# Layer 0's output product by seven quarter products, with later weights rounded in half units

## The chip, the cores and the metric

One core of a Trainium2 chip runs the whole kernel. The metric is device time in microseconds: the median of three runs, 1159.79 us before the change (1158.65 to 1168.03). Engines are named as in the profile: PE multiplies matrices, DVE and ACT do the elementwise work, POOL does a little of it and issues DMAs, SP issues DMAs.

## What is computed

A decoder trunk of two layers over 512 tokens of 1024 features, in float32. Layer 0 mixes tokens with a state-space group and a stick-breaking attention group, layer 1 with a conformer convolution. Each mixer, and each feed-forward network (FFN) behind it, is added to a scaled residual and normalized:

```python
def sqrelu_mlp(x, w1, b1, w2, b2):
    return jnp.square(jax.nn.relu(x @ w1 + b1)) @ w2 + b2

        x = layer_norm(DEEPNORM_ALPHA * x + mix, ln1_g[layer], ln1_b[layer])
        ffn = sqrelu_mlp(x, ffn_w1[layer], ffn_b1[layer], ffn_w2[layer], ffn_b2[layer])
        x = layer_norm(DEEPNORM_ALPHA * x + ffn, ln2_g[layer], ln2_b[layer])
```

The FFN goes from 1024 to 4096 features and back. The change is in the FFN of layer 0 and in how weights of layer 1 are prepared meanwhile.

## The kernel before, in words

**Numbers.** Every operand of a matmul is held as a rounded high part and a low part (`hi`, `lo`; `split` casts on ACT and subtracts on DVE), and each product is three matmuls: high by high, high by low, low by high (`gemm`, L258). Features lie on partitions and tokens along the free axis; the residual `X[j]` is eight tiles of 128 × 512.

**FFN of layer 0, before.** It runs in four blocks of 8 hidden tiles (`FFN_BLOCKS[0]`). A hidden tile (`ffn1`; PSUM tile `f`, in the first block `fl`) is 24 matmuls of 512 columns; then Relu on ACT, a square on DVE and a split into `hh` and `hl`. After each of the first three blocks, `accum` makes 8 output tiles (`acf`) of 24 matmuls of 512 columns and adds them to `X`. The last block's output is made by `Tail` (`tlb`): 16 products of 24 matmuls of 256 columns, 8 output tiles for the first half of the tokens, 8 for the second, the weight of each output tile used in both halves.

**LN b.** `tail_norm_lead` weaves that tail with the layer norm behind it and with the first products of what follows (leads; here `pl`, four of the convolution's first pointwise product, `pw1`). Per token half: sums over the tiles (`sb`), their mean by a matmul with ones (`mpb`), subtraction, squares, sums of squares (`sqb`), their mean (`vpb`), scaling, and the split normalized tiles (`xbh`, `xbl`). The leads of a half follow. LN a, behind the mixer, has the same form with six leads (`fl`) that are the first hidden tiles of layer 0's FFN.

**Weights.** Class `Weights` prepares units (a raw load by SP, cast on ACT, L112, subtraction on DVE, L113) into slots in a fixed order, a few ahead of their use. 30 units of layer 1 (16 of `pw1`, 8 of `pw2`, 6 of the FFN's first matrix, 128 × 1024 each) are prepared in the same slots during layer 0's FFN and stored to DRAM by SP (`keep`: `kepth`, `keptl`); the convolution reloads them, split, through POOL's queue (L97).

**FFN of layer 1, before and after.** It has blocks of 6, 6, 6, 6 and 8 hidden tiles. For the blocks of six, `pair` turns two hidden tiles into seven operands `ah`, `al` (by token half and hidden tile of the pair), `load_quads` loads the output weights as four quarters (`quad`), `operand` forms their differences in place, and `seven` (L1400) makes seven quarter products in place of eight, in the order 1, 2, 5, 6, 3, 7, 4; some share a PSUM bank with the one that they are added to. `turn` closes the pools of the convolution and opens this layer's: slots `s1` to `s4`, `w` for the quarters, `a0` to `a2` for the operands, `q`. A tile of a new pool waits for the tiles that had its place.

**What sets the order.** The program is written in one order and a scheduler places each engine's instructions by priority; each engine then runs its own list strictly in order, and so does each DMA queue. Pages (`page`, 24 of 128 × 512) are taken in turn, and a page is given out again when its last reader is done.

Of the kernel before, what the change touches and what calls it, by code (L numbers as in the profile page):

```python
# [9 lines left out]
F32 = mybir.dt.float32  # L10
# [29 lines left out]
FFN_BLOCKS = ((8, 8, 8, 8), (6, 6, 6, 6, 8))  # L40
# [7 lines left out]
KEEP_FROM = 8  # L48
# [11 lines left out]
class Weights:  # L60


    def __init__(self, tc, ahead):
        self.tc, self.nc, self.ahead = tc, tc.nc, ahead
        self.slots, self.units, self.raw, self.urgent, self.fence, self.hold = [], [], None, True, None, False
        self.done, self.got, self.chunk, self.ready, self.kept = 0, 0, {}, {}, {}
        self.turn, self.quads, self.base = None, {}, 0
# [19 lines left out]
    def _prep(self, n):  # L87
        nc = self.nc
        while self.done < min(n, len(self.units)):
            key, src, nk, ncol, off, width = self.units[self.done]  # L90
            if self.turn and self.done == self.turn[0]:
                self.turn[1]()
            pool, s = self.slots[(self.done - self.base) % len(self.slots)]
# [12 lines left out]
            hi = pool.tile([P, nk, ncol], F32R, tag=f"whi{s}", name=f"whi{self.done}", bufs=1)  # L106
            lo = pool.tile([P, nk, ncol], F32R, tag=f"wlo{s}", name=f"wlo{self.done}", bufs=1)
# [33 lines left out]

    def keep(self, i):

        w = self.next()
        self.kept[i] = tuple(self.tc.dram_tile([P, *w[0].shape[1:]], F32, name=f"kept{x}{i}") for x in "hl")
        for x, d in zip(w, self.kept[i]):
            self.nc.sync.dma_start(d, x.bitcast(F32))
# [51 lines left out]
def kernel(ctx: ExitStack, tc: tile.TileContext, a: dict, out: bass.AP):  # L199
# [13 lines left out]
    X = [const([P, T], f"X{j}") for j in range(KT)]  # L213
# [49 lines left out]
    wst = ExitStack()  # L263
    wpool = wst.enter_context(tc.tile_pool(name="mw", bufs=1))
# [600 lines left out]
    wp2 = wst.enter_context(tc.tile_pool(name="w2", bufs=1))  # L865
    hst = ExitStack()
    hid = hst.enter_context(tc.tile_pool(name="hid", bufs=1, side="right"))
# [11 lines left out]
    def hpage(name, dt=F32R, w=T):  # L879
        return hid.tile([P, PAD + T + 2], dt, tag="hid", name=name, bufs=16)[:, :w]  # L880

    def tmp(name, dt=F32):
        return hid.tile([P, T], dt, tag="tmp", name=name, bufs=8)
# [6 lines left out]
    for j in range(0, D, 128):  # L890
        later += units_of("pw1", a["conv_w_pw1"][0], 0, 8, [j], 256)
        later += units_of("pw1", a["conv_w_pw1"][0], 0, 8, [D + j], 256)
    later += units_of("pw2", a["conv_w_pw2"][0], 0, 8, range(0, D, 128), 256)
    later += units_of("f1l", a["ffn_w1"][1], 0, 8, range(0, LEAD * P, 128), 256)

    kept = [k for j in range(0, 16, 4) for k in (j, j + 2, j + 1, j + 3)] + list(range(16, 24 + LEAD))
    keep_at, n = {}, 0
    for layer in range(2):
        if layer:
            units += [(("split", i), None, 8, 128, 0, 0) for i in range(24 + LEAD)]  # L900
            at_turn = len(W.units) + len(units)
        k0 = 0
        for nb in FFN_BLOCKS[layer]:
            if layer:
                units += units_of("f11", a["ffn_w1"][1], 0, 8, range(max(k0, LEAD) * P, (k0 + nb) * P, 128), 128)
                if nb == NB:
                    units += [(("quad", k0, i), None, nb // 2, T, 0, 0) for i in ORDER7]
                else:
                    for c in (0, T):
                        for k, n_ in ((0, 3), (3, 3), (6, 2)):  # L910
                            src = a["ffn_w2"][1][(k0 + k) * P : (k0 + k + n_) * P, c : c + T].rearrange("(k p) n -> p k n", p=P)
                            units.append((("f21", k0 + k, c), src, n_, T, 0, T))
                k0 += nb
                continue
            for m in range(k0, k0 + nb, 4):
                units += units_of("f10", a["ffn_w1"][0], 0, 8, range(m * P, min(m + 4, k0 + nb) * P, 128), 256)
                if m >= KEEP_FROM:
                    keep_at["f", m + 3] = kept[n : n + 2]
                    units += [later[i] for i in kept[n : n + 2]]
                    n += 2  # L920
            for j in range(0, KT, 4):
                units += units_of("f20", a["ffn_w2"][0], k0, nb, range(j * P, (j + 4) * P, 128), 256)
                if k0 + nb < 32:
                    m = 4 if j else 2
                    keep_at["a", k0, j + 3] = kept[n : n + m]
                    units += [later[i] for i in kept[n : n + m]]
                    n += m
            k0 += nb
    W.add_slots(wp2, 5)
# [78 lines left out]
    class Tail:  # L1008


        def __init__(self, xk, ln, bias):
            self.xk, self.ln, self.bias, self.done = xk, ln, bias, 0
            self.ws = [W.next() for _ in range(len(xk))]
            W.fence = None
# [51 lines left out]
    def tail_norm_lead(xk, name, bias, g, b, lead_n, lead_name, then=None, early=0):  # L1066

        ln = LN(name)
        t = Tail(xk, ln, bias)
# [10 lines left out]
    def ffn1(layer, bi, k0, nb, xs, fps, first=()):  # L1080
        hs = []
        for i in range(nb):
            m = k0 + i
            if i < len(first):
                ps = first[i]
            else:
                ps = fps(f"f{layer}{m}")
                gemm(ps, W.next(), slice(0, P), xs, 0, T)
# [3 lines left out]
            pg_ = page if (i < 4) == (bi % 2 == 0) else hpage  # L1092
            hh, hl = pg_(f"hh{layer}{m}"), pg_(f"hl{layer}{m}")
            split(hh, hl, r)
            hs.append((hh, hl))
            for k in keep_at.get(("f", m), ()) if layer == 0 else ():
                W.keep(k)
        return hs


# [6 lines left out]
    xs, first = tail_norm_lead(cat[4:8], "a", rb[0], ("ln1_g", 0), ("ln1_b", 0), LEAD, "fl0")  # L1107
    wdw = hid.tile([P, KT, CONV], F32, tag="wdw", name="wdw")
    mask = hid.tile([P, 32], F32, tag="mask", name="mask")

    def taps():
        for f in range(2):
            wn = tmp(f"wn{f}")[:CONV]
            nc.sync.dma_start(wn, a["conv_w_dw"][0][:, f * T : (f + 1) * T])
            ps = stp(f"wd{f}")
# [17 lines left out]

    acc = [None] * KT
# [380 lines left out]
```

## Time and profile before

| | us |
|---|---|
| median of three runs | 1159.79 |
| profiled execution, its time | 1164.9 |
| span of the profiled execution | 1163.2 |
| PE busy | 1133.7 |
| DVE busy | 820.6 |
| ACT busy | 550.0 |

The mean granted clock of PE was 0.994. The time of the profiled execution is 1.7 us over its span, which runs from the first to the last recorded instruction. Busy times overlap between engines; what PE's busy time leaves of the span, 29.5 us, is all the time in which no matmul ran. In the views of the profile, `L258` is a line of the kernel before, an arrow in `out<-in` stands between what an instruction writes and reads, and `x192` counts instructions.

### The profile page before, as it was taken

Reading aid. Unit: us, or ns where it says so; the run is one execution under the profiler, and the core shown is the slowest. Engines: PE = TensorE matmul, PEld = TensorE weight load, DVE = VectorE, ACT = ScalarE, POOL = GpSimd, SP = SyncE. Lnnn points to the kernel's source line nnn. Section 1 sums busy time; section 2 is a strip of 40 time slices with the busy share of each in tenths; the row PEclk is TensorE's granted clock in tenths of the full one; section 3 lists DMA queues with packets and bytes.
Section 4 is the critical chain, followed back from the end, with each engine's and each line's share of the span. In section 5 each row is a group of like instructions: output and inputs, shape, how many; then the busy total and the mean of one; then the engine's idle time right before and its main releaser. Section 6 shows DMA issues by size and latency. Waiting matters only on the chain.

```text
span 1163.2 us, 17835 instructions
## 1 busy us (share of the span) xinstructions
PE 1133.7 (97%) x7156; PEld 948.5 (82%) x7156; DVE 820.6 (71%) x1401; ACT 550.0 (47%) x838; POOL 70.2 (6%) x125
## 2 busy tenths in 40 slices
PE   9989989999999999999999999999999999999997
PEld 7777767799888888888899867689988888888885
DVE  7999865578645645645647699988695958588337
ACT  7857759435524524523513231364673536263530
POOL 1022221000000000000002211002000000000000
PEclk9999989999999999999999999999999999999999
DMA  9621212150878778788617634156024151515211
GB/s 204 173 63 50 74 56 74 55 181 14 267 244 289 250 273 282 267 268 274 217 46 245 226 137 146 39 170 227 4 82 135 50 151 44 172 35 156 65 54 73
DMA packets 145907, 169.59 MB, mean 146 GB/s; under 512 B 13922, under 2 KB 119138, under 8 KB 145824
## 3 DMA queue, kind: packets, MB, share of 16 engines
q1 hardware_dynamic: 137024, 136.96, 37.1%
q0 software_dynamic: 8640, 31.46, 8.0%
q8 instruction: 56, 0.92, 0.3%
q14 instruction: 27, 0.22, 0.1%
q10 hardware_dynamic: 160, 0.03, 0.0%
HBM read 132.12 MB, written 35.65 MB: 144 GB/s over the span
## 4 chain that ended last, share of the span: by engine, by line
PE 78%; DMA 6%; DVE 6%; ACT 5%; issue 2%; SPq 2%; POOL 1%; DVEq 0%; ACTq 0%
PE f L258 20%; PE acf L258 10%; PE s L1400 10%; DMA raw<-in_ffn_w_dram 4%; PE tld L258 4%; PE h L1445 4%; PE tlb L258 4%; PE fl L258 3%; PE pv L258 3%; PE cw L1174 3%; PE pg L258 3%; PE tla L258 2%; PE acmo L258 2%; DVE wlo L113 2%; PE pl L258 2%
## 5 line engine op out<-in xcount | busy, mean ns | idle before, releaser
L112 ACT CAST whi<-raw 128x1024 fp32r<-128x1024 f32 (+1 forms) x150 | 156.6, 1061 | 259.1 <-PE acf L258 66.3
L113 DVE TENSOR_TENSOR wlo<-raw,whi 128x1024 fp32r<-128x1024 f32 (+1 forms) x150 | 183.6, 1236 | 122.1 <-ACT whi L112 122.1
L258 PE MATMUL f<-xah,whi 128*128 128x512 f32 x208 | 81.0, 390 | 0.0
L258 PE MATMUL f<-xal,whi 128*128 128x512 f32 x208 | 81.0, 389 | 0.0
L258 PE MATMUL f<-xah,wlo 128*128 128x512 f32 x208 | 80.9, 389 | 0.0
L258 PE MATMUL f<-xdh,whi 128*128 128x512 f32 x208 | 80.9, 389 | 0.0
L258 PE MATMUL f<-xdl,whi 128*128 128x512 f32 x208 | 80.9, 389 | 0.0
L258 PE MATMUL f<-xdh,wlo 128*128 128x512 f32 x208 | 80.9, 389 | 0.0
L258 PE MATMUL acf<-hl,whi 128*128 128x512 f32 x192 | 75.8, 395 | 0.1
L258 PE MATMUL acf<-hh,wlo 128*128 128x512 f32 x192 | 75.7, 394 | 0.0
L258 PE MATMUL acf<-hh,whi 128*128 128x512 f32 x192 | 75.3, 392 | 0.0
L1400 PE MATMUL s<-whi,al 128*128 128x512 f32 x168 | 65.0, 390 | 0.0
L1400 PE MATMUL s<-wlo,ah 128*128 128x512 f32 x168 | 64.9, 390 | 0.0
L1400 PE MATMUL s<-whi,ah 128*128 128x512 f32 x168 | 64.5, 392 | 0.0
L113 DVE TENSOR_TENSOR wlo<-quad,whi 128x1536 fp32r<-128x1536 f32 x28 | 49.1, 1754 | 7.6 <-ACT whi L112 7.5
L391 DVE SCALAR_TENSOR_TENSOR cy<-hp,wdw,cy 128x512 f32<-128x512 f32 (+1 forms) x75 | 49.5, 660 | 0.5 <-ACT cy L187 0.5
L112 ACT CAST whi<-quad 128x1536 fp32r<-128x1536 f32 x28 | 41.0, 1483 | 17.2 <-PE f L258 8.0
L97 POOL DMA_DIRECT2D whi<-kepth x30 | 16.0, 535 | 547.6 <-PE tlb L258 386.7
L258 PEld LDWEIGHTS f<-xdh,whi 128*128 128x128 f32 x208 | 39.0, 188 | 8.1
L258 PEld LDWEIGHTS f<-xah,wlo 128*128 128x128 f32 x208 | 39.0, 188 | 8.1
L258 PEld LDWEIGHTS f<-xah,whi 128*128 128x128 f32 x208 | 39.0, 188 | 8.1
L258 PEld LDWEIGHTS f<-xdl,whi 128*128 128x128 f32 x208 | 39.0, 188 | 8.1
(647 smaller groups left out, 3064.4 us busy)
## 6 DMA issues: line engine op xcount, KB each, us to landing
raw<-in_ffn_w_dram SPq DMA_DIRECT2D x35, 1024.0 KB, 6.0
kepth<-whi SPq DMA_DIRECT2D x30, 512.0 KB, 4.4
keptl<-wlo SPq DMA_DIRECT2D x30, 512.0 KB, 9.5
whi<-kepth POOLq DMA_DIRECT2D x30, 512.0 KB, 3.6
wlo<-keptl POOLq DMA_DIRECT2D x30, 512.0 KB, 4.4
raw<-in_ffn_w_dram SPq DMA_DIRECT2D x28, 512.0 KB, 4.0
raw<-in_conv_w_pw_dram SPq DMA_DIRECT2D x12, 1024.0 KB, 6.7
quad<-in_ffn_w_dram SPq DMA_DIRECT2D x16, 768.0 KB, 4.6
```

Source lines behind the costliest of these rows:

```text
L97: nc.gpsimd.dma_start(x, d)
L112: i0 = nc.scalar.copy(hi, raw).ins
L113: i1 = nc.vector.tensor_sub(lo, raw, hi.bitcast(F32)).ins
L258: ins = PE.matmul(ps[:, c0:c1], u[:, k, ksl], v[:, c0:c1], start=start and k == 0 and i == 0, stop=stop and k == n - 1 and i == 2).ins
L391: V.scalar_tensor_tensor(o, x, s, y, op0=op0, op1=op1)
L1174: PE.matmul(cps[j, c0][g][C, :], Ds[j][t // 16][R, t % 16, :], hps[j][R, t + c0 : t + c1], start=t < 4, stop=t >= n - 4, tile_position=(R. ...
L1400: PE.matmul(ps, u, v[:, p, :], start=chain == i and p == 0 and n_ == 0, stop=p == len(As) - 1 and n_ == 2, skip_group_check=True)
L1445: PE.matmul(ps, u, v, start=k == 0 and i == 0, stop=k == nb_last - 1 and i == 2)
```

## The change

Layer 0's FFN takes the blocks of layer 1, 6, 6, 6, 6 and 8, and its first four blocks the seven products.

- **Products.** `seven_by_feature` makes them with the weights as the stationary operand, so that the result comes out with features on partitions, in PSUM tiles `z` of 128 × 512 that hold two feature tiles of one token half: per block 7 × 36 = 252 matmuls of 256 columns. The first block's product 1 starts a sum `R1` (two pages) that is added to half of `X` during the last block; the other results are added to `X` directly (`region`).
- **Hidden tiles.** `pair` serves both layers; Relu and Square write `q` in place on ACT. The last block's hidden tiles go to the places of `a0` to `a2`.
- **Pools.** `quarters(0)` opens layer 0's pools behind LN a; `plain`, called when the first unit of the convolution's weights is prepared, lays `tmp one hid four two three` over them, with 12 tiles in `tmp`. `tmp` (sums and squares of LN b among them) begins where `s1` and `s2` lie. The first four output weights of the last block are put into places of `w` and `q` (`in_quads`, `in_q`), the other four into the slots.
- **Later weights.** `half_units` loads the 30 later units in 60 halves of 256 KB into pages (`kr`), splits them (`kh`, `kl`) and stores both parts, all three DMAs issued by POOL. `keep` does one half: 7 in the first block, 13 in each of the next three, 14 in the last.
- **Residual.** `X` is scaled and gets its bias in eight ACT instructions ahead of the FFN, instead of the bias in each addition; the transposes of the convolution's taps (`taps`) are taken in two steps of block 0.

The core of the diff:

```diff
+    def half_units():
+        raws = {}
+        def load(n):
+            if n < 2 * (24 + LEAD):
+                (w, c), h = later[n // 2], n % 2
+                raws[n] = page(f"kr{n}", F32)
+                G.dma_start(raws[n].rearrange("p (k n) -> p k n", k=4), w[4 * h * P : 4 * (h + 1) * P, c : c + P].rearrange("(k p) n -> p k n", p=P))
+        load(0)
+        for n in range(2 * (24 + LEAD)):
+            load(n + 1)
+            hi, lo = page(f"kh{n}"), page(f"kl{n}")
+            split(hi, lo, raws.pop(n))
+            for d, x in zip(W.kept[n // 2], (hi, lo)):
+                G.dma_start(d[:, 4 * (n % 2) : 4 * (n % 2) + 4, :], x.bitcast(F32).rearrange("p (k n) -> p k n", k=4))
+            yield
...
-            r = tmp(f"fr{layer}{m}")
-            act(r, ps, AF.Relu, bias=pv("ffn_b1", 32 * layer + m))
-            tt(r, r, r, ALU.mult)
...
+            ps = pss[e] if pss else hidden(layer, m + e, xs)
+            x = q[:, 1:3] if e else q[:, 0:8:7]
+            act(x, ps.rearrange("p (h c) -> p h c", h=2), AF.Relu, bias=pv("ffn_b1", 32 * layer + m + e))
+            act(x, x, AF.Square)
+            if then:
+                then()
...
+    ORDERS = ("s1 s2 raw s3 a1 s4 a2 a0 q w", "s1 s2 raw w a1 s4 a2 b q s3 a0")
...
+    def plain():
+        wst[0].close()
+        wst[0] = ExitStack()
+        p = opened("tmp one hid four two three".split())
+        room.update(tmp=p["tmp"], hid=p["hid"], bufs=12)
+        W.slots, W.count, W.raw, W.ahead = [], 0, None, 5
+        for x, n in (("three", 3), ("two", 2), ("one", 1), ("four", 4)):
+            W.add_slots(p[x], n)
...
+    for j in range(KT):
+        act(X[j], X[j], AF.Identity, bias=rb[1][:, j : j + 1], scale=ALPHA)
+    R1 = [page(f"R1{b}", F32) for b in range(2)]
...
+    def seven_by_feature(k0, As, first, bi):
+        bank, opened = {}, None
+        for n, i in enumerate(ORDER7):
+            wh, wl = W.next()
+            chain = CHAIN.get(i, i)
+            for b in range(2):
+                if chain == i:
+                    bank[i, b] = nps(f"z{k0}{i}{b}")
+                ps = bank[chain, b]
+                for d in range(2):
+                    c = slice((2 * b + d) * P, (2 * b + d + 1) * P)
+                    for p, (ah, al) in enumerate(As):
+                        uh, ul = ah[:, PLACE[i]], al[:, PLACE[i]]
+                        for n_, (u, v) in enumerate(((wh, uh), (wh, ul), (wl, uh))):
+                            opens = chain == i and p == 0 and n_ == 0
+                            ins = PE.matmul(ps[:, d * H : (d + 1) * H], u[:, p, c], v, start=opens and d == 0,
+                                            stop=p == len(As) - 1 and n_ == 2, skip_group_check=True).ins
...
+            for b in range(2):
+                ps = bank[chain, b]
+                if i == 1:
+                    if first:
+                        S.copy(R1[b], ps)
+                    else:
+                        tt(R1[b], R1[b], ps, ALU.add)
+                else:
+                    x = region({2: 0, 5: 3, 6: 1, 3: 1, 7: 3, 4: 2}[i], b)
+                    tt(x, x, halves(ps), ALU.add)
+            keep()
...
-    for bi, nb in enumerate(FFN_BLOCKS[0]):
-        if bi == 1:
-            taps()
-        hs = ffn1(0, bi, k0, nb, xs, nps, first if bi == 0 else ())
-        if bi < len(FFN_BLOCKS[0]) - 1:
-            accum(nps, hs, f"f0{bi}", 1024 // nb, bi == 0, keep=lambda j: keep_at.get(("a", k0, j), ()))
+    for bi, nb in enumerate(FFN_BLOCKS[:-1]):
+        if bi:
+            W.load_quads(k0, a["ffn_w2"][0], k0, nb)
+        As = []
+        for m in range(k0, k0 + nb, 2):
+            As.append(pair(0, m, xs, first[m : m + 2] if bi == 0 else None, keep if bi else None))
+        seven_by_feature(k0, As, bi == 0, bi)
         k0 += nb
-    xs, first = tail_norm_lead(hs, "b", rb[1], ("ln2_g", 0), ("ln2_b", 0), 4, "pl")
+    hs, ws = [], []
+    for i in range(FFN_BLOCKS[-1]):
+        if i % 3 == 0:
+            hl_ = [f1[f"a{i // 3}"].tile([P, 3, T], F32R, tag=f"a{x}", name=f"h0{x}{i}", bufs=1) for x in "hl"]
+        r = rect(0, k0 + i, hidden(0, k0 + i, xs))
+        act(r, r, AF.Square)
+        hs.append(tuple(x[:, i % 3, :] for x in hl_))
+        split_part(*hs[-1], r)
+        if i < 4:
+            ws.append(W.next())
+        x = region(i // 2, i % 2)
+        tt(x, x, halves(R1[i % 2]), ALU.add)
+        keep(2 - (i > 5))
+    xs, first = tail_norm_lead(hs, "b", None, ("ln2_g", 0), ("ln2_b", 0), 4, "pl", ws=ws)
```

How the instructions stand on the engines, at three places. A number behind a name (`tlb_5603`) tells one tile from another, and lines are those of the kernel that the rows are of. First PE around LN b, before the change: the last product ahead of the first half's mean and the first behind it, and the same for the variance.

```order
L258 MATMUL tlb_5603<-hh_5315,wlo_5211 128x256
L956 MATMUL mpb_5629<-sb_5423,ones 128x256
L258 MATMUL tlb_5662<-hh_5037,whi_5246 128x256
...
L258 MATMUL tlb_5717<-hh_5315,wlo_5320 128x256
L956 MATMUL vpb_5744<-sqb_5632,ones 128x256
L258 MATMUL tlb_5776<-hh_5037,whi_5329 128x256
```

PE there in the change, from the end of the tail's last product on:

```order
L257 MATMUL tlb_6748<-h0h_6118,whi_6210 128x256
L257 MATMUL tlb_6748<-h0l_6119,whi_6210 128x256
L257 MATMUL tlb_6748<-h0h_6118,wlo_6211 128x256
L982 MATMUL mpb_6520<-sb_6314,ones 128x256
L982 MATMUL vpb_6635<-sqb_6523,ones 128x256
L257 MATMUL pl_6775<-xbh_6478,whi_6242 128x256
L257 MATMUL pl_6833<-xbh_6478,whi_6246 128x256
```

Before, 216 tlb products stand ahead of `mpb`, 72 between it and `vpb`, and 96 behind that; in the change all 384 stand ahead of both.

Second, DVE in the first half of LN b, before the change: the tail's evacuations (`X<-tlb`) and the sums `sb`.

```order
L391 SCALAR_TENSOR_TENSOR X_61<-tlb_5371,rb_2541,X_61 128x256
L391 SCALAR_TENSOR_TENSOR X_62<-tlb_5397,rb_2541,X_62 128x256
L387 TENSOR_TENSOR sb_5423<-X_61,X_62 128x256
L391 SCALAR_TENSOR_TENSOR X_63<-tlb_5425,rb_2541,X_63 128x256
L387 TENSOR_TENSOR sb_5423<-sb_5423,X_63 128x256
```

And in the change; `tlb_6721` and `tlb_6748` are the tail's 15th and 16th products, `D` diagonals of the convolution.

```order
L387 TENSOR_TENSOR X<-tlb_6694,X 128x256
L387 TENSOR_TENSOR X<-tlb_6721,X 128x256
L1332 TENSOR_TENSOR D_7040<-mask,wdw 128x512
L1332 TENSOR_TENSOR D_7041<-mask,wdw 128x256
L387 TENSOR_TENSOR sb_6314<-X 128x256
L387 TENSOR_TENSOR X<-tlb_6748,X 128x256
L387 TENSOR_TENSOR sb_6314<-sb_6314,X 128x256
L1307 MEMSET hp_7044 128x30
L387 TENSOR_TENSOR sb_6314<-sb_6314,X 128x256 x5
L387 TENSOR_TENSOR X<-X,mpb_6520 128x256 x8
```

The first sum stood behind the second evacuation and stands now behind the 15th; the other six stand behind the 16th.

Third, DVE at the start of block 0 in the change; `q` and `al` belong to the operands of the last pair, `wlo` from a `quad` is one of the seven weight operands, `kl` a half unit.

```order
L387 TENSOR_TENSOR q_3426<-q_3426 128x256
L1207 COPY wdw<-wd_3496 128x124
L118 TENSOR_TENSOR wlo_3223<-quad_3214,whi_3222 128x1536
L118 TENSOR_TENSOR wlo_3227<-quad_3216,whi_3226 128x1536
L138 TENSOR_TENSOR quad_3214<-quad_3218,quad_3214 128x1536
L1120 TENSOR_TENSOR al_3428<-q_3426,ah_3427 128x768
L387 TENSOR_TENSOR q_3426<-q_3426 128x256
L142 TENSOR_TENSOR quad_3218<-quad_3220,quad_3218 128x1536
L118 TENSOR_TENSOR wlo_3232<-quad_3214,whi_3231 128x1536
```

All seven weight operands and the four differences stand behind the last pair's first difference, which needs the last lead's square.

More of the change, by code (lines that the diff above doesn't have):

```diff
@@ L211, in page @@
         return pgp.tile([P, T], dt, tag="pg", name=name, bufs=24)
[L213 removed]
+    Xall = const([P, KT, T], "X")
+    X = [Xall[:, j, :] for j in range(KT)]
     ident = const([P, P], "ident")
@@ L890 @@
     for j in range(0, D, 128):
[L891 to L897, printed above, removed]
-    for layer in range(2):
+        later += [(a["conv_w_pw1"][0], c) for c in (j, D + j)]
@@ L902 @@
[L902 to L927, printed above, removed]
-            k0 += nb
@@ L1078, in tail_norm_lead, with rect @@
         return xs, lead.finish()
[L1080 to L1088, printed above, removed]
-            r = tmp(f"fr{layer}{m}")
-            act(r, ps, AF.Relu, bias=pv("ffn_b1", 32 * layer + m))
-            tt(r, r, r, ALU.mult)
[L1092 to L1098, printed above, removed]
+    def rect(layer, m, ps):
+        r = page(f"r{layer}{m}", F32)
+        act(r, ps, AF.Relu, bias=pv("ffn_b1", 32 * layer + m))
+        return r
@@ new lines, with opened, quarters, turn @@
+    PLACE = {1: 0, 2: 1, 4: 2, 5: 3, 6: 4, 7: 5, 3: 6}
+    CHAIN = {3: 5, 7: 6, 4: 6}
+    f1 = {}
+    wm = ExitStack()
+    ORDERS = ("s1 s2 raw s3 a1 s4 a2 a0 q w", "s1 s2 raw w a1 s4 a2 b q s3 a0")
+    def opened(names, **kw):
+        return {x: wst[0].enter_context(tc.tile_pool(name=f"{x}{len(W.units)}{W.done}", bufs=1, reuse_waits="tile", **kw)) for x in names}
+    def quarters(layer):
+        def turn():
+            if layer:
+                wm.close()
+            wst[0].close()
+            wst[0] = ExitStack()
+            room.clear()
+            f1.clear()
+            f1.update(opened(ORDERS[layer].split()))
+            W.slots, W.count, W.raw, W.ahead = [], 0, f1["raw"], NSLOT - 1
+            for x in ("s1", "s2", "s3", "s4"):
+                W.add_slots(f1[x], 1)
+            W.quad = f1["w"]
+            W.load_quads(0, a["ffn_w2"][layer], 0, NB)
+        return turn
```

185 lines of the change are left out of this document (113 added, 72 removed).

## The prediction

> **What bounds the kernel now.** I read the page first, then the chain of waits, then windows over single stages, then the rows of LN b and of the costs.
>
> ```profile
> span 1163.2 us, 17835 instructions
> PE 1133.7 (97%) x7156; PEld 948.5 (82%) x7156; DVE 820.6 (71%) x1401; ACT 550.0 (47%) x838; POOL 70.2 (6%) x125
> ```
>
> PE is busy for 97% of the span: only 29.5 us are without a matmul. So whatever takes products away shortens the kernel only if no new idle time of PE appears, and whatever makes PE wait counts in full.
>
> ```profile
> 401.94 44.59 PE acf L258 x192
> 446.53 43.52 PE f L258 x192
> ...
> 582.37 22.52 PE tlb L258 x187
> 604.89 0.43 PE mpb L956 x2
> 605.32 8.56 PE tlb L258 x72
> 613.89 0.43 PE vpb L956 x2
> 614.32 11.42 PE tlb L258 x96
> 625.73 2.88 PE pl L258 x24
> ...
> 639.32 11.09 PE pl L258 x92
> 650.41 5.24 PE pv L258 x23
> ```
>
> Each row is start, duration, engine, tile, line, count. In layer 0's FFN the chain runs through PE row upon row: a hidden block (f), an output block (acf), a hidden block. In LN b, mean (mpb) and variance (vpb) of the first token half lie between tlb products of the second half, and the leads (pl) of the first half follow at once: the norm's first half is hidden under the tail.
>
> ```profile
> 358.00:402.00 44.00, 44.00 (x197) 36.41 (x196) 27.55 (x33) 22.65 (x29) 0.00 (x0) 1.00 0.84 285
> 578.00:626.00 48.00, 47.06 (x392) 46.69 (x391) 29.36 (x69) 9.68 (x21) 7.64 (x15) 1.00 0.42 143
> 883.00:945.00 62.00, 62.00 (x274) 50.95 (x273) 45.68 (x49) 29.10 (x32) 0.00 (x0) 1.00 0.35 103
> ```
>
> The columns after the stretch and its length are busy time of PE, weight loads, DVE, ACT and POOL, the granted clock, the DMA share and GB/s. PE is full in a hidden block of layer 0 (row 1), in the tail with 256-column products (row 2, where weight loads are nearly full as well), and in a seven-product block of layer 1 (row 3). The others have room; DVE has least of it, in row 3, the pattern that layer 0 now takes over.
>
> **The change, part by part.** First, the products. Removed are three acf blocks of 192 matmuls of 512 columns, by the chain's row 44.59 each: 133.8 us. Added are four blocks of 252 matmuls of 256 columns. Their nearest rows are the tlb rows: (22.52 + 8.56 + 11.42) / (187 + 72 + 96) = 0.1197 us each; 1008 × 0.1197 = 120.7. Hidden products, tail and leads keep their number. PE work falls by **13.1 us**, and this can't be more than 16.8, which half a 512-wide matmul (0.2322 / 2) would make of it; the weight loads, one to a matmul in row 2, speak against that.
>
> Second, LN b. By the order of the change the first sum of LN b's first half (sb) comes on DVE behind the 15th of 16 tlb evacuations, and PE issues all 384 tlb before mpb. The sum's tile lies where the weight of the tail's seventh tile lies, which is read once more by the 15th product. So the norm's first half can't lie under the second half of the tail. Its length stands in the second half of before, where nothing covered it:
>
> ```profile
> 626.29 0.42 DVE L387 TENSOR_TENSOR sb<-sb,X 128x256 f32<-128x256 f32 x1
> 629.08 2.73 DVE L387 TENSOR_TENSOR X<-X,mpb 128x256 f32<-128x256 f32 x8 [2.37 <-PE mpb L956]
> 631.74 2.55 DVE L387 TENSOR_TENSOR sqb<-sqb,sqb 128x256 f32<-128x256 f32 x7
> 635.89 0.42 DVE L391 SCALAR_TENSOR_TENSOR tb<-vpb,rb 128x256 f32<-128x256 f32 x1 [1.60 <-ACT rb L193]
> 637.27 1.28 DVE L391 SCALAR_TENSOR_TENSOR X<-X,PV,rb 128x256 f32<-128x256 f32 x3
> ...
> 628.45 0.59 PE L956 MATMUL mpb<-sb,ones 128*128 128x256 f32 x2
> 638.35 0.74 PE L258 MATMUL pl<-xbh,whi 128*128 128x256 f32 x4 [0.26 <-ACT xbh L187]
> ```
>
> The chain from mpb (628.45) to the first lead of that half (638.35) takes 9.9 us. Call the end of the last tlb T. After T follow, in the change, one evacuation at 0.42, six sums that depend on each other at 0.42 (some 3 us with their starts), then the 9.9, and 1.1 more for the second half's sums that DVE does in between, with 0.9 for the two hand-overs: the first lead starts at T + 14.9, and PE has nothing to do until then. 96 lead products at 0.12 are 11.5, so they end at T + 26.4. The clock adds to that:
>
> ```profile
> 159.45 1.12 PE L757 MATMUL av<-w2C,vt 128*64 128x256 f32 x2 [4.41 <-POOL w2C L706]
> 160.00:162.00 2.00, 1.17 (x4) 0.29 (x2) 0.00 (x0) 0.38 (x1) 0.29 (x1) 0.50 0.00 0
> 164.00:168.00 4.00, 4.00 (x25) 3.55 (x24) 1.12 (x4) 3.42 (x7) 0.39 (x2) 0.72 0.00 0
> ```
>
> After 4.41 us of idle PE the granted clock is 0.50, and its mean over 164 to 168 still 0.72: 1.1 us are lost in these four, and about as much before; I take 1.9, so T + 28.3. The second half's mpb, behind the first half's chain on DVE (its last rows end near T + 20.9), has the same 9.9 behind it: T + 30.8 for the first lead of that half, and with another 11.5 and its start T + 42.9 for the last. Before, this took from 625.73 to 650.41, 24.7. The loss is **18 us**; at the least 15 (the uncovered chain alone, the second half hidden whole), at the most 22.
>
> The Trainium skill (TensorE: Matmul & The Clock Gate, section Part 1: The HAM clock gate) has the clock fall after a window of about 3.4 us without work. By this rule the second gap of LN b, 2.5 us, keeps the full clock and my sum stands; by the row alone, which shows only a longer gap, it may fall again and cost another 1.9.
>
> Third, the start of block 0. The order puts 32 DVE instructions between the first weight split and product 7's first evacuation, behind the last lead's square. Their prices:
>
> ```profile
> L113 DVE TENSOR_TENSOR wlo<-raw,whi 128x1024 fp32r<-128x1024 f32 x146 | 176.6, 1222 | 107.2 <-ACT whi L112 107.1
> L113 DVE TENSOR_TENSOR wlo<-quad,whi 128x1536 fp32r<-128x1536 f32 x28 | 49.1, 1754 | 7.6 <-ACT whi L112 7.5
> L249 DVE TENSOR_TENSOR hl<-fr,hh 128x512 fp32r<-128x512 f32 x32 | 22.0, 689 | 12.4 <-ACT hh L248 12.4
> L387 DVE TENSOR_TENSOR X<-X,s 128x512 f32<-128x512 f32 x48 | 31.9, 682 | 11.9 <-PE s L1400 11.9
> L137 DVE TENSOR_TENSOR quad<-quad,quad 128x1536 f32<-128x1536 f32 x4 | 7.0, 1756 | 0.1
> L1367 DVE TENSOR_TENSOR al<-q,ah 128x1024 fp32r<-128x1024 f32 x12 | 14.7, 1222 | 6.7 <-ACT ah L1366 6.7
> L187 ACT ACTIVATE X<-X,rb 128x512 f32<-128x512 f32 x16 | 10.2, 719 | 0.0
> ```
>
> Seven operand splits 12.3, four operand differences 7.0, two raw splits 2.4, two parts of al 2.2, nine evacuations 6.1, five half units (kl, priced as hl) 3.4, three short differences 1.3: 34.8 us. Product 4 follows on PE with 4.3, so the block ends 39.1 after DVE's start; PE has 252 × 0.1197 = 30.2 of its own, and 9 products of the next block that it does meanwhile (2.1). That leaves 6.8 of waiting. I take **6**, since the queue can start a little ahead of PE; from 0 (PE itself late by its last pair, DVE ahead) to 10 (the operands' loads late too). The eight scalings of X on ACT (0.72 each, in the leads) are within it.
>
> Fourth, the later weights. What moves:
>
> ```profile
> kepth<-whi SPq DMA_DIRECT2D x30, 512.0 KB, 4.4
> whi<-kepth POOLq DMA_DIRECT2D x30, 512.0 KB, 3.6
> ...
> 880.00:890.00 10.00, 10.00 (x45) 8.29 (x45) 4.09 (x6) 2.59 (x4) 0.00 (x0) 1.00 0.46 132
> 1050.00:1060.00 10.00, 10.00 (x46) 8.29 (x45) 10.00 (x14) 2.84 (x3) 0.00 (x0) 1.00 0.77 244
> 520.00:530.00 10.00, 10.00 (x45) 8.12 (x44) 3.51 (x5) 2.10 (x2) 0.00 (x0) 1.00 0.99 372
> ```
>
> 60 stores of 512 KB leave SP; 60 half loads and 120 half stores of 256 KB come to POOL's queue, ahead of the 60 reloads there, which are needed only from LN b on. The same bytes are cast and subtracted, in pieces of 512 columns. In blocks 1 to 3, 13 pieces each add 13 × 0.689 = 9.0 to DVE's 45.7 of row 3: 54.7 of some 63 us, so PE's products hide them. A piece holds three of six free pages from its load to the end of its stores; at about 3.7 us each, 13 take 48, hidden as well. In the last block the cover is thin: eight hidden tiles are 43.5 us on PE, 16 weights of 0.524 MB and 14 loads of 0.262 are 12.06 MB, by row 880 (132 / 0.46 = 287 GB/s with rows of 512 bytes) 42 us, and 28 stores of 0.262 by row 520 (372 / 0.99 = 376) 20: 62. Of these some 16 may lie ahead or behind (the first weights are preloaded, the tail's last ones and stores come later), so 46 against 43.5. And the last hidden tile's split stands on DVE behind the last piece's: a late load or page there holds the tail. I take **5 us**, from 0 (all hidden) to 20 (the 62 in full, with the next block's start).
>
> The Trainium skill (DMA: Bandwidth & Descriptors, section Specifications) counts rows of 512 bytes as enough for full rate. By this the loads go as fast as the wider rows at 1050 (244 / 0.77 = 317 GB/s), the last block's transfers fit under its products, and the sum is about 3 lower; the trace has 287, and I keep to it.
>
> R1's additions in the last block (8 of 0.68) lie under hidden products, Relu and Square in place cost ACT what the separate ones did.
>
> **Sum**: −13.1 + 18 + 6 + 5 = **+15.9**. The profiled execution took 1164.9 (span 1163.2), so it would take 1180.8; it lies 5.1 over the median of the three runs, and on the median 1159.79 the forecast is **1175.7 us**, slower by 1.4%.
>
> **Rivals.** A: the only new wait is LN b's uncovered chain at its least, 15, and block 0 and the pieces hide: −13.1 + 15 = +1.9, **1161.7 us**, no change. For it: ACT and the DMA queues have much room, and layer 1 runs the same blocks with PE full (row 883). Against: in layer 1 there are no pieces, and other work covers the first operands. B: pieces and weights bind in the last block, by DMA or by pages: the fourth term at 20, +30.9, **1190.7 us**. For it: one queue issues 180 transfers, in order, each waiting for its page or its split. Against: the rate of 376 at row 520 shows reserves. C, the other side: the sums do not wait, and run tile by tile under the tail as before. What decides is whether the sum's tile must be free of the seventh weight. Since PE's own order has no tlb behind mpb, mpb then comes at T, the first lead at T + 10.5 (0.6 and 9.9), the second half's first at T + 23, and the last at T + 35.5: the loss shrinks from 18 to 10.8, and with block 0 and the pieces hidden the time is 1159.8 − 13.1 + 10.8 = **1157.5**, not slower; with z at its lower bound 1153.8. For it: order shows rows and not waits. Against: the sum's first row stands behind the 15th evacuation there, where before it stood behind the second.
>
> **Chances.** Forecast 0.45, A 0.28, B 0.19, C 0.08. A difference of 1% (11.6 us) is about what a measurement of this kernel can tell. Of the forecast's 0.45, with its own bounds, 0.39 lies over 1171.4 and 0.06 below; A gives 0.26 to no change and 0.02 to slower, B all to slower, C 0.05 to no change and 0.03 to faster, this if the second half's chain hides too. Faster 0.03, same 0.37, slower 0.60. The range is 1160 to 1197: it takes in most of A and all of B but its end, and leaves out C (0.08), A's lower part (0.08) and the worst of B (0.04).
>
> **What would show it.** Right, if in the profile after z takes about 0.12 us a matmul; if tlb runs in one piece of 384 and PE is then idle for about 15 us, with a lower granted clock at the first pl; if PE waits for DVE (wlo, from quad) in block 0 by some 6 us and is full in blocks 1 to 3; and if the last hidden tile waits a few us behind kl. Wrong, if mpb lies within 1 us of the last tlb (then C), if PE waits in blocks 1 to 3 for kl, a page or a weight load (then B, and the term was set too low), or if z takes well over 0.12.

## The result, and the profile after

The change makes the kernel slower: 1246.51 us median (1245.26 to 1250.16, four runs) against 1162.96 before, a ratio of 1.0722 with a 95% interval of 1.0664 to 1.0780. The forecast was 1175.7 with a range from 1160 to 1197: the direction was right, the size was not.

The page after, span and busy time:

```profile
span 1243.6 us, 19229 instructions
PE 1156.3 (93%) x7588; PEld 981.8 (79%) x7588; DVE 899.2 (72%) x1505; ACT 600.7 (48%) x914; POOL 176.5 (14%) x305
```

PE is without a matmul for 87.3 us (1243.6 − 1156.3) where it was 29.5. And its busy time rose by 22.6, though it has some 12 us less to multiply: the same matmuls took longer, and the mean granted clock was 0.966 in place of 0.994.

The chain of waits around LN b; the rows of before stand in the prediction, and T is again the end of the tail's last product:

```profile
629.57 45.03 PE tlb L257 x357
678.47 2.73 DVE X L387 x8
681.21 2.01 DVE sqb L387 x6
688.63 7.49 PE pl L257 x48
696.56 5.75 PE pl L257 x48
705.75 1.22 PE pl L257 x4
707.39 11.83 PE pl L257 x92
719.22 5.24 PE pv L257 x23
```

The tail runs in one piece, then DVE is the chain, and the first lead comes at 688.63, 14.0 us after the last product (629.57 + 45.03 = 674.60). The second half's first lead is at T + 31.1 and its last ends at T + 44.6; predicted were 14.9, 30.8 and 42.9. Before, the same stretch took 24.7, so LN b costs 19.9 here.

But 719.22 stands against 650.41 before: 68.8 us later, of which LN b explains 20. The rest was lost earlier. Windows over block 1's products and block 2's hidden tiles (columns as before: PE, weight loads, DVE, ACT, POOL, clock, DMA share, GB/s):

```profile
380.00:390.00 10.00, 6.26 (x35) 5.91 (x35) 9.24 (x11) 5.42 (x8) 3.12 (x5) 0.74 0.38 131
390.00:400.00 10.00, 10.00 (x79) 10.00 (x79) 8.37 (x10) 4.77 (x4) 0.00 (x0) 0.92 0.46 151
400.00:410.00 10.00, 10.00 (x86) 10.00 (x85) 8.45 (x11) 3.16 (x4) 3.44 (x6) 1.00 0.90 291
410.00:420.00 10.00, 8.27 (x51) 7.73 (x50) 5.24 (x8) 3.85 (x5) 4.88 (x8) 0.83 1.00 308
420.00:430.00 10.00, 10.00 (x46) 8.27 (x45) 3.95 (x5) 2.80 (x5) 4.83 (x9) 1.00 0.96 301
430.00:440.00 10.00, 7.17 (x31) 5.61 (x30) 2.95 (x5) 3.95 (x7) 3.87 (x7) 0.97 0.77 246
```

From 390 to 400 POOL issues nothing and DVE is nearly full, with the block's operands; from 400 to 430 the transfers fill the DMA (0.90 to 1.00), from 410 on DVE and ACT are idle for about half of the time or more, and PE has pauses. Rows of the timeline show what POOL, and then ACT, wait for there (in brackets the idle time before and what ended it):

```profile
403.86 0.54 POOL L912 DMA_DIRECT2D keptl<-kl  x1 [16.09 <-DVE kl L248]
```

```profile
426.98 0.62 ACT L247 CAST kh<-kr 128x512 fp32r<-128x512 f32 x1 [2.33 <-DMA kr<-in_conv_w_pw_dram]
427.51 1.05 ACT L117 CAST whi<-raw 128x1024 fp32r<-128x1024 f32 x1
```

For 16 us the pieces stand still behind the operands' work on ACT and DVE. Then 11 of them follow between 403 and 444, one in 4.0 us; before seven of their casts ACT waits for the load. The cast of the next hidden tile's weight (`whi`) stands in ACT's line behind the piece's cast. The table of waits over the FFN (engine, line, what it waited for; us in total, times, longest) has the sum, and below it what PE waited for there most:

```profile
DVE kl L248 <- ACT kh L247: 53.6, 27, 4.7
ACT kh L247 <- DMA kr<-in_conv_w_pw_dram: 47.4, 20, 4.6
ACT kh L247 <- DMA kr<-in_ffn_w_dram: 17.7, 9, 4.1
PE z L1238 <- ACT ah L1119: 12.6, 5, 3.7
PE f L257 <- ACT q L185: 10.8, 7, 3.2
PE f L257 <- ACT r L185: 6.1, 1, 6.1
```

So PE waits for operands, Relus and squares of ACT, and ACT waits for the loads of pieces.

One more loss lies where the change was thought to move nothing, ahead of layer 1's block 0. The chain there, and ACT's first Relu in that block:

```profile
908.10 11.53 PE fl L257 x96
...
930.77 30.74 PE s L1504 x126
```

```profile
919.65 1.27 ACT L185 ACTIVATE q<-fl,PV 128x512 f32<-128x512 f32 x2 [9.57 <-PE fl L257]
```

The leads end at 919.63 and the first product starts 11.1 us later, where before 3.65 us of transposes lay between them (from 851.26 to the start of `s` at 854.92). ACT had nothing to do for 9.57 us and started when the last lead was done, though this Relu reads the first.

### The profile page after: what moved, and what is told of

It reads as the page before. It is cut to its first block, busy times and chain, and to the rows that moved or that the text cites. A ratio compares the mean times of both kernels' runs of the same rounds, so it can differ in the third digit from the quotient of the medians.

```text
span 1243.6 us, 19229 instructions
## 1 busy us (share of the span) xinstructions
PE 1156.3 (93%) x7588; PEld 981.8 (79%) x7588; DVE 899.2 (72%) x1505; ACT 600.7 (48%) x914; POOL 176.5 (14%) x305
## 4 chain that ended last, share of the span: by engine, by line
PE 59%; issue 10%; DVE 6%; ACT 5%; DMA 5%; POOL 4%; SPq 0%; DVEq 0%; POOLq 0%; ACTq 0%
PE f L257 12%; PE s L1504 10%; PE fl L257 5%; PE tlb L257 4%; PE h L1549 4%; PE tld L257 4%; PE z L1238 3%; PE pv L257 3%; PE pg L257 2%; PE cw L1324 2%; PE pl L257 2%; PE tla L257 2%; PE acmo L257 2%; POOL kr L904 2%; DMA kepth<-kh 2%
## 5 line engine op out<-in xcount | busy, mean ns | idle before, releaser
L117 ACT CAST whi<-raw 128x1024 fp32r<-128x1024 f32 (+1 forms) x92 | 97.8, 1066 | 163.7 <-PE s L1504 47.8
L118 DVE TENSOR_TENSOR wlo<-raw,whi 128x1024 fp32r<-128x1024 f32 (+1 forms) x92 | 114.3, 1247 | 83.3 <-ACT whi L117 83.1
L1238 PE MATMUL z<-ah,whi 128*128 128x256 f32 x336 | 98.5, 302 | 20.1 <-ACT ah L1119 12.6
L118 DVE TENSOR_TENSOR wlo<-quad,whi 128x1536 fp32r<-128x1536 f32 x56 | 98.0, 1753 | 8.0 <-ACT whi L117 7.8
L1238 PE MATMUL z<-al,whi 128*128 128x256 f32 x336 | 97.9, 295 | 0.8 <-DVE al L1120 0.8
L1238 PE MATMUL z<-ah,wlo 128*128 128x256 f32 x336 | 97.1, 293 | 0.0
L248 DVE TENSOR_TENSOR kl<-kr,kh 128x512 fp32r<-128x512 f32 x60 | 41.4, 690 | 70.9 <-ACT kh L247 53.6
L1238 PEld LDWEIGHTS z<-ah,whi 128*128 128x128 f32 x336 | 67.8, 207 | 23.0 <-ACT ah L1119 13.6
L1238 PEld LDWEIGHTS z<-al,whi 128*128 128x128 f32 x336 | 68.1, 203 | 1.6 <-DVE al L1120 1.2
L1238 PEld LDWEIGHTS z<-ah,wlo 128*128 128x128 f32 x336 | 67.7, 202 | 0.0
```

The lines of the kernel that those rows point to most:

```text
L117: i0 = nc.scalar.copy(hi, raw).ins
L118: i1 = nc.vector.tensor_sub(lo, raw, hi.bitcast(F32)).ins
L248: i1 = V.tensor_sub(lo, src, hi.bitcast(F32)).ins
L1238: ins = PE.matmul(ps[:, d * H : (d + 1) * H], u[:, p, c], v, start=opens and d == 0, stop=p == len(As) - 1 and n_ == 2, skip_group_check=T ...
```

## The experiments

Theory Q: the half units (pieces below) stall PE, because ACT and DVE stand in line behind a piece whose load is late. LN b's uncovered chain and the pause ahead of layer 1 are losses of their own. All times are medians of four to ten runs; ratios are to the kernel before, measured beside each (its medians were 1160.2 to 1163.9).

**No pieces.** Edit: `keep` does nothing, and the reloads read other weights.

```diff
-        for _ in range(n):
-            next(half_unit, None)
+        pass
```

> Leaves out the half units: no load, split or store of later weights during layer 0's FFN; the convolution reloads other weights of the same size and row length. Theory Q (ACT and DVE stand in line behind pieces whose load is late, so PE waits): PE's waits in blocks 1 to 4 go, LN b's gap stays, about 1187 us (1246.5 less 55 to 65). Rival Z (the seven products, their operands and pools cause the waits): at least 1220 us.

Measured: 1190.09 us, ratio 1.0241 (1.0206 to 1.0276). The pieces cost 56 us. The window over the block shown above, with the pieces and without:

```profile
400.00:465.00 65.00, 56.70 (x306) 49.27 (x305) 43.66 (x53) 31.60 (x42) 26.56 (x44) 0.93 0.78 248
```

```profile
400.00:465.00 65.00, 64.11 (x401) 58.00 (x400) 46.52 (x50) 29.33 (x32) 0.00 (x0) 1.00 0.32 99
```

PE does 401 matmuls there in place of 306, at full clock. The chains show where the 56 us lie. In the change the last block's hidden tiles and, behind LN b, `pv` start at

```profile
569.33 5.48 PE f L257 x24
...
719.22 5.24 PE pv L257 x23
```

and without pieces at

```profile
527.98 43.34 PE f L257 x191
...
662.52 5.24 PE pv L257 x23
```

The leads ahead of block 0 start within 0.2 us of each other in the two. So 41 us are lost in blocks 0 to 3, and 15 in the last block and its tail.

**Transfers alone.** Edit: no cast and no subtraction, both stores take the raw page.

```diff
-            split(hi, lo, raws.pop(n))
-            for d, x in zip(W.kept[n // 2], (hi, lo)):
+            x = raws.pop(n)
+            for d in W.kept[n // 2]:
```

> Keeps all 180 transfers of the half units from the same queue and their pages, but leaves out cast and subtraction; both stores take the raw page, so that the later weights are wrong. Theory Q: nothing on ACT and DVE waits for a piece any more, so as without pieces, 1185 to 1195 us. Rival D (the transfers take bandwidth or the queue from the FFN's own weights): 1230 us or more.

Measured: 1200.39 us, ratio 1.0333 (1.0289 to 1.0376). The same window:

```profile
400.00:465.00 65.00, 62.09 (x375) 56.05 (x374) 44.92 (x48) 29.30 (x31) 31.48 (x53) 0.97 0.93 301
```

The DMA share is higher than in the change (0.93 against 0.78), and yet PE runs. A busy DMA alone costs 10 of the 56 us. By the tables of waits, PE waits for ACT in the FFN 7 us here, 34 in the change and 2.5 without pieces. One thing more differs: a piece holds one page here, and three in the change, so fewer transfers have to wait for a page.

**Casts and subtractions alone.** Edit: all pieces split one page that is loaded once; no stores.

```diff
-            load(n + 1)
-            split(hi, lo, raws.pop(n))
+            split(hi, lo, raws[0])
...
-            for d, x in zip(W.kept[n // 2], (hi, lo)):
```

> Keeps the 60 casts and 60 subtractions, from one page that is loaded once, and leaves out the other 59 loads and all stores of the half units; the convolution reloads other weights. Theory Q: the pieces never wait, so at most 5 us over the kernel without pieces, about 1190 us. Rival S (the work of the pieces on ACT and DVE, 60 times 0.62 and 0.69 us, is what PE waits for): 1225 us or more.

Measured: 1189.17 us, ratio 1.0230 (1.0208 to 1.0252): as without pieces. The 120 instructions on ACT and DVE cost nothing when nothing makes them wait. Neither half of a piece is dear; the other 46 us come only with both, when work that waits for a transfer stands in the lines of engines that PE waits for. Whether it waits for its load or for a page that a store has yet to leave, these three runs do not tell apart.

**LN b in pages.** Edit: sums, squares (two to a page) and root of the first half in free pages.

```diff
-                    self.s[c0, 0] = tmp(f"s{self.n}{c0}")[:, c0:c1]
+                    self.s[c0, 0] = (page(f"s{self.n}{c0}", F32) if self.n == "b" and c0 == 0 else tmp(f"s{self.n}{c0}"))[:, c0:c1]
```

> The change with one edit: the first half's sums, squares and root of LN b lie in free pages instead of the tiles over the tail's weights. PE's order then has mpb and vpb between tlb products again. If the uncovered chain costs what the prediction says: 18 us less, 1228 us. Rival: the leads of the first half then wait for their weights instead, and the gain is under 6 us, over 1240 us.

Measured: 1227.55 us, ratio 1.0558 (1.0529 to 1.0586), 19 us less. Its chain is that of before again, with mean and variance inside the tail and no pause ahead of the leads:

```profile
632.58 24.33 PE tlb L257 x189
657.34 8.63 PE tlb L257 x72
666.41 11.51 PE tlb L257 x96
677.92 3.72 PE pl L257 x31
```

**q behind the convolution's pool.** The placement in memory gave the suspicion: layer 1's first `q` began at byte 185856 of a partition, and the place of the last lead's low weight ended at 186048. Edit: the pool ahead of `q` is 384 bytes longer.

```diff
-    sts = [f1["b"].tile([P, 9, 12], F32, tag="bst", name=f"bst{b}", bufs=4)
+    sts = [f1["b"].tile([P, 11, 12], F32, tag="bst", name=f"bst{b}", bufs=4)
```

> The change with the pool b of layer 1 made 384 bytes longer, so that q lies behind the convolution's last pool instead of reaching 192 bytes into the place of the last lead's weight. Theory O (layer 1's first Relu waits 9.6 us for the last lead only because of this overlap): PE's pause ahead of block 0 of layer 1 goes back from 11 to about 4 us, about 1237 us. Rival (Relu in place, or ACT's order, holds it): no gain, 1244 us or more.

Measured: 1232.63 us, ratio 1.0619 (1.0580 to 1.0657), 14 us less by the medians and 12 by the ratios. The first Relu runs while the leads do, and PE has transposes right behind them:

```profile
905.15 1.27 ACT L185 ACTIVATE q<-fl,PV 128x512 f32<-128x512 f32 x2 [0.54 <-PE fl L1084]
```

```profile
905.47 11.52 PE fl L257 x96
916.99 3.49 PE xt L1483 x32
920.48 29.14 PE s L1504 x126
```

So 192 bytes of overlap held layer 1 for 7.5 us of pause, and the products behind it ran slower at first (30.74 against 29.14). These rows account for 9 us; the rest of the 14 is not traced to a place, and the intervals of the two ratios are wider than it.

**Products alone.** The three edits above together (no pieces, LN b in pages, `q` behind).

> No half units (as in the run without pieces), LN b's sums in free pages, and q behind the convolution's pool: of the change only the seven products, their operands and pools stay. If the three losses are all there is and add up: 1246.5 - 56 - 19 - 9 = 1162 us. By the prediction's terms for products and block 0 alone (-13.1 + 6): 1154 us. Rival (something else in layer 0's pools still costs): over 1168 us.

Measured: 1160.84 us, ratio 1.0007 (0.9988 to 1.0025): the three losses add up (56 + 19 + 14 = 89, or 84 with the 9 of the rows; measured 86), and what is left, the seven products with their operands and without the work for the later weights, is no faster than before.

```profile
span 1158.7 us, 18661 instructions
PE 1126.9 (97%) x7588; PEld 963.2 (83%) x7588; DVE 862.4 (74%) x1445; ACT 569.5 (49%) x854; POOL 66.6 (6%) x125
```

It has the same 7588 matmuls as the change and is busy with them for 29.4 us less. Of the 84.9 us between the two spans, 55.5 are idle time of PE and 29.4 are slower matmuls; the mean granted clock was 0.994 here and 0.966 there.

**Pieces on POOL.** Edit: cast and subtraction of the pieces on POOL.

```diff
-            split(hi, lo, raws.pop(n))
+            raw = raws.pop(n)
+            G.tensor_copy(hi, raw)
+            G.tensor_sub(lo, raw, hi.bitcast(F32))
```

> The change with cast and subtraction of the half units on POOL instead of ACT and DVE; transfers, pages and their order stay. Theory Q (the loss is ACT and DVE standing in line behind a piece whose load is late): the pieces wait among themselves, and it takes what the kernel with transfers alone takes, 1200 us, up to 1215 if POOL's slower work delays the last pieces. Rival (the pieces are too slow as a chain, wherever they run, and the end of the last block waits for them): 1235 us or more.

Measured: 1242.46 us, ratio 1.0694 (1.0654 to 1.0734): the time that the rival gave, and not theory Q's. But the edit brought a cost of its own: DVE became slower while POOL computed. The same group of DVE in the change and here:

```profile
L387 DVE TENSOR_TENSOR q<-q 128x256 f32<-128x256 f32 x96 | 40.2, 420 | 11.2 <-ACT q L185 10.1
```

```profile
L387 DVE TENSOR_TENSOR q<-q 128x256 f32<-128x256 f32 x96 | 58.0, 606 | 11.3 <-ACT q L185 10.1
```

PE's waits show both. Those ahead of hidden tiles fell from 16.9 us in the change to 3.9, as theory Q has it; those ahead of the products rose from 20.4 to 33.1, as the operands came later from the slower DVE. And in the last block, from 589 to 613 us, the chain runs through pieces on POOL, as the rival has it. So the time of this run decides nothing on the line of waits; that POOL is no place for this work, it does show.

**The same with both other edits.**

> All of the change with three edits: half units on POOL, LN b's first half in free pages, q behind the convolution's pool; it computes the reference. If the gains add up: 1200 - 19 - 9 = 1172 us. If POOL's pieces keep the last block waiting: 1185 us or more.

Measured: 1210.45 us, ratio 1.0422 (1.0361 to 1.0483): 32 less than the run before it, as LN b and `q` together should give, and no more; of the two answers expected, it is the one in which the pieces on POOL stay dear. Of the kernels here that leave out no work it is the fastest, and still slower than the kernel before.

**Three edits of the pieces' own chain.** Three runs: loads issued by SP; loads two pieces ahead, from POOL; and loads two pieces ahead with the low part written over the raw page (two pages a piece). The excerpt shows the edits one after another; with loads two ahead, a second load also goes ahead of the loop.

```diff
-                G.dma_start(raws[n].rearrange("p (k n) -> p k n", k=4), w[4 * h * P : 4 * (h + 1) * P, c : c + P].rearrange("(k p) n -> p k n", p=P))
+                nc.sync.dma_start(raws[n].rearrange("p (k n) -> p k n", k=4), w[4 * h * P : 4 * (h + 1) * P, c : c + P].rearrange("(k p) n -> p k n", p=P))
...
-            load(n + 1)
+            load(n + 2)
...
-            hi, lo = page(f"kh{n}"), page(f"kl{n}")
-            split(hi, lo, raws.pop(n))
+            raw, hi = raws.pop(n), page(f"kh{n}")
+            lo = raw.bitcast(F32R)
+            split(hi, lo, raw)
```

> The change with one edit: the 60 loads of half units are issued by SP; stores stay on POOL. If a load is late because it stands in POOL's queue behind stores that wait for a cast: 1215 us or less. If a load is late because no page is free, or because it is issued one piece ahead only: 1235 to 1250 us.

> The change with one edit: the load of a half unit is issued two pieces ahead instead of one, from the same queue and the same six pages. If a load's 4.9 us are longer than one piece's turn and that is what ACT waits for: 1215 us or less. If pages or the queue's order hold it: over 1235 us.

> As the run with loads two pieces ahead, and the low part is written over the raw page, so that a piece holds two pages instead of three. If pages are what is missing: 1205 to 1215 us, well below the run with loads two ahead. If the queue's order or the place of the pieces in ACT's and DVE's order is: at most 10 us below it.

Measured: 1243.63 (ratio 1.0690, 1.0635 to 1.0745), 1251.38 (1.0781, 1.0740 to 1.0823) and 1240.86 us (1.0690, 1.0645 to 1.0735). None of the three is the missing thing. The third run is 10.5 us below the second, where 1215 or less was expected if pages were what is missing. A piece that no longer waits for its load waits for its page. From the third run's waits:

```profile
ACT kh L247 <- DMA keptl<-kr: 62.1, 25, 5.3
```

ACT's casts of pieces waited 65 us for loads in the change, and 62 us for stores here.

**Fewer bytes.** Without the stores of the low parts, and, apart from it, without the loads but the first.

```diff
-            for d, x in zip(W.kept[n // 2], (hi, lo)):
+            for d, x in zip(W.kept[n // 2][:1], (hi,)):
```

```diff
-            load(n + 1)
...
-            split(hi, lo, raws.pop(n))
+            split(hi, lo, raws[0])
```

> The change without the stores of the low parts (512 KB a piece instead of 768); the convolution reloads other weights as low parts, all else stays. If the bytes of the pieces fill the DMA and make their turns long: about a third to a half of the 56 us comes back, 1215 to 1228 us. If the place of the pieces in the order decides: 1238 us or more.

> The change without the loads of the half units but the first, which all pieces then split; both stores stay (512 KB a piece). If ACT and DVE wait for pages that come back with the stores: 1220 us or more. If they wait for loads: 1190 to 1200 us.

Measured: 1227.04 us, ratio 1.0550 (1.0506 to 1.0594), and 1209.44 us, ratio 1.0394 (1.0358 to 1.0431). A third of the bytes less gives back 20 of the 56 us if it is a store, some 37 if it is the load: both stand in a piece's turn. The first time lies where it was expected if the bytes make the turns long. The second expectation had two answers, and 1209 lies between them: without loads, ACT's casts still waited 29 us for stores.

**Spread.** 10 pieces in each of blocks 1 to 3 in place of 13, 8 in the last block, and 15 under the first half of the tail.

```diff
-            if then:
+            if then and not e:
                 then()
...
-        keep(2 - (i > 5))
+        keep()
...
+                if self.ln.n == "b" and h == 0:
+                    keep(2)
```

> All 60 pieces with all their transfers, spread otherwise: 7, 10, 10, 10 and 8 in the blocks and 15 under the first half of the tail, where DMA and ACT are idle. If the pieces are too many for the time that a block leaves them: 1246.5 less 25 to 45, 1200 to 1222 us. If each piece costs the same wherever it stands: no gain in the blocks, 1240 us or more.

> The spread run with LN b's first half in free pages and q behind the convolution's pool; it computes the reference. If the gains add up: 25 to 30 us below the spread run, 1175 to 1195 us. If the pieces under the tail hold LN b: as the spread run less the 14 of q.

Measured: 1228.83 us, ratio 1.0577 (1.0537 to 1.0617), and 1222.76 us with the two other edits, ratio 1.0514 (1.0489 to 1.0539). The place of the pieces is worth some 17 us with all their bytes, less than the 25 expected. With the other edits only 6 more came, where 25 to 30 were expected if the gains add up: a piece under the tail brings its wait along, and LN b's squares on ACT then stand behind it, as the chain of that run shows.

```profile
664.04 5.07 DMA kr<-in_ffn_w_dram
669.71 1.34 ACT sqb L185 x4
```

## Why the prediction was wrong, point by point

- **Products, −13.1.** About right. In the run without pieces a stretch of 212 `z` takes 25.70 us, 0.1212 each instead of 0.1197, so 1008 of them take 122.2 where the three `acf` blocks took 133.8: −11.6.
- **LN b, +18.** Right in mechanism and size: 19 by the run in pages, 19.9 by the chain. The second pause was 3.4 us instead of 2.5, and the clock fell behind it as well.
- **Block 0, +6, and the rest of layer 0.** The wait is there, and smaller: in the run with the products alone, PE is idle for 3.8 of the 39.2 us that end with block 0, where before it was idle for 0.1 of 59.3. Blocks 1 to 3 add 2.9 us of idle PE that the sum did not have. −11.6 + 3.8 + 2.9 would be −4.9, and the kernel is level with before (+0.8 us, −1.4 to +2.9). The rest is not traced to a place.
- **Later weights, +5 with bounds 0 to 20.** This is the step that failed; measured 56. The bounds were made for the last block, and the 15 us lost in it and in its tail lie within them. The other 41 lie in blocks 0 to 3, for which the term held nothing: blocks 1 to 3 take 75 to 76 us each in the change, and 64 to 65 without pieces. Three things in the term were wrong. It set 13 pieces at 3.7 us, for which it shows no row and which is near the 4.0 measured, against a whole block of 63 us and called them hidden; in fact the order keeps them behind the operands' work in the first part of the products, and some 11 of them fall into 41 us. It looked for the bound in bandwidth and pages; transfers alone, with one page a piece, cost 10. And it looked for a stall only in the last block, and there only at one row of DVE, while in every block the piece's cast waits for a transfer in ACT's line, with the next weight's cast and the next Relu behind it. The wait that the change adds was priced as if the engine could go on.
- **What was not in the sum.** The layout of layer 1's pools, +14 by the medians, of which rows show 9. The diff changes the order and sizes of the pools there, and I read it as moving nothing.
- **The clock.** I added 1.9 us for one pause, and there it is about right: the first 48 leads took 7.49 us and the next 48 took 5.75. But it falls behind many of the other pauses too, and 29.4 us of the loss are matmuls that ran slower, at a lower granted clock in the mean.
- **The rivals.** B named the right work with too small a price (1190.7), and put all of it into the last block; what it spoke of, DMA and pages, is nearest to the run with transfers alone. The sign that the prediction gave for its being wrong came true in part: PE waits in blocks 1 to 3, though for ACT's operands and Relus, and not itself for `kl`, a page or a load. A and C did not happen: PE's order held, and the uncovered chain was there in full.

## What to carry to other kernels

Work that must wait for a transfer does not belong in the in-order line of an engine that feeds the critical one, even if that engine is idle for half of the time, as ACT is here (48% busy): price it by what stands behind it while it waits, not by its own duration. Count background pieces against the stretch into which the order puts them, not against the whole stage. When pools are laid over each other, compare the byte ranges of the first tiles with the last tiles under them; here 192 bytes of overlap were enough for a wait.

## What the runs showed of the hardware

A pause of PE costs more than its length. Around LN b of the change:

```profile
680.00:684.00 4.00, 0.06 (x1) 0.06 (x1) 4.00 (x13) 1.66 (x6) 0.00 (x0) 0.50 1.10 398
...
688.00:692.00 4.00, 3.37 (x16) 3.37 (x16) 4.00 (x12) 2.83 (x6) 0.00 (x0) 0.50 0.00 0
692.00:696.00 4.00, 4.00 (x35) 4.00 (x35) 1.98 (x5) 1.02 (x2) 0.00 (x0) 1.00 0.02 6
...
706.00:710.00 4.00, 4.00 (x22) 3.90 (x23) 4.00 (x11) 1.86 (x6) 0.00 (x0) 0.62 0.00 0
```

The leads start at 688.63 at half clock and do 16 matmuls to 692, then 35 in the next four microseconds. Behind the second pause, from 702.3 to 705.75, the clock is down again (0.62). Shorter pauses had the same behind them in the blocks: after 1.73 us without a matmul, to 414.76, the clock was 0.50 from 416 to 418, and after 2.83 us, to 437.89, it was 0.50 from 440 to 442. It was back at 1.00 from 419 and from 443 on.

The Trainium skill (TensorE: Matmul & The Clock Gate, section Part 1: The HAM clock gate) gives a window of about 3.4 us both for the fall and for the return. For the return this trace agrees: it took from 688.63 to about 692. For the fall it does not: 1.73 and 2.83 us were enough. So the prediction's second pause of 2.5 us could have cost clock as well, where it let the sum stand by that rule.

POOL's elementwise work slowed DVE: with the pieces on POOL the mean of 96 subtractions of 256 columns rose from 420 to 606 ns. Of these, 39 that lie between 300 and 640 us, beside POOL's work, went from 419 to 877 ns, and the 48 of layer 1, without it, stayed at 421.
